# Where the last of five weight matrices made ahead is finished: in the mixer projection's second half, or behind the sixth query tile

## The chip, the core and the metric

The kernel runs on one core of a Trainium2 chip. The metric is the device time of one execution in microseconds; the time before is the median of three runs, 1076.35 us (1072.25 to 1078.3). TensorE multiplies matrices, VectorE (DVE) and ScalarE (ACT) work elementwise, GpSimd (POOL) does small vector work and issues some transfers, SyncE (SP) issues the other transfers. Each engine takes its instructions in one fixed order; an instruction that waits holds up all behind it on that engine.

## The reference

One layer of a hybrid decoder runs over 512 prompt tokens and 64 sample tokens (8 sequences of 8), 576 columns in all, with the same weights. All is float32.

```python
u = _rms(x) * g_pre_mix
proj = u @ w_in                                   # -> Mamba-2 heads and mLSTM heads
mix = jnp.concatenate([y_ssd, h_ml], axis=-1) @ w_out       # 2048 -> 1024
x = x + _rms(mix) * g_post_mix
u = _rms(x) * g_pre_x
qx = u @ w_xq                                     # 1024 -> 1024, 4 heads of 256
o = softmax(qx @ mem_k.T / 16) @ mem_v @ w_xo     # cross-attention on 256 memory rows
x = x + _rms(o) * g_post_x
u = _rms(x) * g_pre_ffn
x = x + _rms((silu(u @ w_gate) * (u @ w_up)) @ w_down) * g_post_ffn
```

For the prompt, `mem_k` and `mem_v` are made in the kernel from `mem_prompt` (normalised, times `w_mem_k`, `w_mem_v`); for the samples they come from a cache. The states of both recurrences are outputs too.

## The kernel before

**Numbers in two parts.** A float32 operand of a product is split in two: a rounded part made by a cast (`whi`, `..._h`), and the remainder made by a subtraction (`wlo`, `..._l`). A product takes three matmuls for each 128 rows of depth: high by high, high weight by low activation, low weight by high activation (L215, L216, L218 of `gemm`). A weight unit is 128 partitions by 1024 columns, 512 KB. `split_w` loads it (SP), casts it (ScalarE, L191) and lowers it (VectorE, sometimes GpSimd, L198); two raw buffers and three pairs of parts take turns.

**Blocks made ahead.** For eight weight units of later stages (`PRE`: two of `wxo`, and three each of `wgate` and `wup`) the remainder is made early, and kept in a DRAM tensor `pre`; the later stage fetches it from there into `wlo` (L1813). The first three units go through other code (`raw_ahead`, `low_ahead`, `store_ahead`). The last five go through `presplit(n, left)`: it finishes blocks until `left` are in flight, and starts `n` new ones. To start is a load `prel` on POOL's queue (L1326) into one of three buffers, which are shared with tiles of the attention (tags `pr`, `prl`, `mv`). To finish is a cast on ScalarE (`preh`, L1320), a subtraction in place on VectorE (`prel`, L1321) and a store on POOL's queue (`pre`, L1322). A block that takes a buffer again waits until the block before has been stored from it.

**The mixer projection's second half.** The output has eight tiles `j` of 128 features, over two groups of tokens: `i = 0`, 256 columns, and `i = 1`, 320 columns. `out2(j, i)` is the product with the second half of the depth, 24 matmuls. For `j` from 0 to 3 both groups are done; for `j` from 4 to 7 first the 320 columns of all four, then the 256 columns from 7 down to 4. The weight of `j = 4` is loaded anew for that. Each product's evacuation (`o2_evac`) adds it to `f` (VectorE, L1441, `f_mix` in the profile), squares the sum on ScalarE (`sq`, L302), adds that up in `ssqo` (VectorE, L303), and scales `f` (ScalarE, L1443). When the 320 columns of all eight tiles are there, `turned_cols` sums `ssqo` over the features (`ps_ss`, L249: three transposes on TensorE); it is queued behind `out2(7, 0)`. The root (`po_v` to `po_r`) and its spread over partitions (`ps_rb`, L287) follow, then `chain2`: norm, residual, and the parts `u2h`, `u2l` of the next activation. In this stage ScalarE and VectorE also prepare the memory rows (`memory`, with `ssqm` and the root `rmem`) and four weight units of the memory's products (`wm_split`). `presplit` is called once in each turn of `j`. A block's cast is queued behind the last evacuation so far (`evs[-1]`).

**The query stage.** `mem_key(3)` and `mem_value(3)` (`ps_mk`, `ps_v`) come first, then `xq(j, 1)` for `j` from 0 to 7: one unit of `wxq` against 320 columns, evacuated by `q_evac` (cast `qh` on ScalarE, L1555; remainder `ql` on VectorE, L1556; for the sample columns a copy `qsm`). Between the tiles stand `chain2` for the other token group, the squares of `x` (`pre_sums`) and two roots. Then comes the attention, head by head. `attn_values` writes the tiles `prh` and `prl`, which use the buffers of `preh` and of the last block `prel`.

**Order.** The program's order gives priorities. A planner with its own timeline simulation writes out each engine's order and assigns buffers; `tc.issue_after(ins)` forces what is traced in it behind `ins` on the same engine.

Of the kernel before, what the change touches and what calls it, by code (L numbers as in the profile page):

```python
# [115 lines left out]
def build(nc, tc, ctx, I, O):  # L116
    V, A, G, S, TE = nc.vector, nc.scalar, nc.gpsimd, nc.sync, nc.tensor
# [24 lines left out]
    def BP(name="b"):  # L142
        return pb.tile([P, 512], F32, name=name, tag="b")
# [77 lines left out]
    def gemm2(units, xh, xl, evac, name, halves=(0, 1), alloc=None, order=None, parts=HALVES):  # L221
        for i in halves:
            t0, n = parts[i]
            ps = (alloc or GP)(name)[:, :n]
            m = gemm(ps, units, xh, xl, t0, n, order=order)
            evac(t0, n, ps)
        return m

    def act(t):
        return lambda k, t0, n: t[:, k, t0:t0 + n]  # L230
# [48 lines left out]
    def rstd_rows(rc, chunks, out, alloc=None, copy=None):  # L279

        for c0 in range(0, len(chunks), 3):
            part = chunks[c0:c0 + 3]
            b = part[0][0]
            w = part[-1][0] + part[-1][1] - b
            ps = (alloc or BP)("ps_rb")
            for j, (t0, n) in enumerate(part):
                rows.append(TE.transpose(ps[:, t0 - b:t0 - b + n], rc[:n, c0 + j:c0 + j + 1].to_broadcast([n, P]),  # L287
                                         ident[:n, :n]))
            (copy or A.copy)(out[:, b:b + w], ps[:, :w])
        return ps  # L290
# [53 lines left out]
    for k in range(KT):  # L344
        if k % 2 == 0:
            c = slice(128 * k, 128 * k + 256)
# [64 lines left out]
    behind, split_behind = {}, {}  # L411
# [341 lines left out]
    for g in range(2):  # L753
        ps = BP("ps_xts")
# [5 lines left out]
    ps = BP("ps_bts")  # L760
# [15 lines left out]
    for g in range(2):  # L776
# [13 lines left out]
        for h in range(8):  # L790
            k, j = h % 2, (8 * g + h) // 2
# [6 lines left out]
    ps = BP("ps_eg")  # L798
# [7 lines left out]
    for b in range(4):  # L806
# [9 lines left out]
        for hb in range(2):  # L816
# [5 lines left out]
            for g in range(2):  # L822
                ps = BP("ps_hu")
# [6 lines left out]
    ps = BP("ps_yt")  # L830
# [206 lines left out]
    for hb in range(2):  # L1037
# [6 lines left out]
        for b in range(4):  # L1044
# [9 lines left out]
            for h in range(4):  # L1054
                ps = BP("ps_cu")
# [50 lines left out]
    def SL0(name, dt=F32R):  # L1106
        return big0.tile([P, KT, T], dt, name=name, tag="s0", bufs=1)
# [69 lines left out]
    evs = []  # L1177
# [116 lines left out]
    def ahead_src(n):  # L1294
        k, j = PRE[n]
        return I[{"xo": "wxo", "g": "wgate", "u": "wup"}[k]][j]
# [14 lines left out]
        with tc.issue_after(p_.low.ins):  # L1311
            S.dma_start(pre[:, n_, :], t_.bitcast(F32))

    def presplit(n, left):

        while len(ahead) > left:
            n_, t_ = ahead.pop(0)
            h_ = at.tile([P, 1024], F32R, name="preh", tag="prh", bufs=1)
            with tc.issue_after(evs[-1].ins):
                A.copy(h_, t_)  # L1320
            V.tensor_tensor(t_, t_, h_.bitcast(F32), op=ALU.subtract)  # L1321
            G.dma_start(pre[:, n_, :], t_)  # L1322
        for _ in range(n):
            n_ = turns.pop(0)
            t_ = at.tile([P, 1024], F32, name="prel", tag=("pr", "prl", "mv")[n_ % 3], bufs=1)
            G.dma_start(t_, ahead_src(n_))  # L1326
            ahead.append((n_, t_))
# [66 lines left out]
    def weights(key, src, n=1024, pool=None, cut=CUT, acc=False):  # L1394

        for kept in recent.values():
            for k, w in kept:
                if k == key:
                    return w
        kept = recent.setdefault(pool, [])  # L1400
        kept.append((key, split_w(src, n, cut, acc, pool)))
        if len(kept) > (NWX if pool else 3):
            kept.pop(0)
        return kept[-1][1]
# [9 lines left out]
    rmem_b = at.tile([P, 256], F32, name="rmem_b")  # L1414
    ssqm, ssq = ssq_tile("ssqm"), ssq_tile("ssqo")
    presplit(1, 0)
    for j in range(4):
        k2 = slice(2 * j, 2 * j + 2)
# [12 lines left out]
    def memory_norm(part, m):  # L1431
        with tc.issue_after(m.ins):
            if not part:
                rmem[0] = turned_cols(ssqm, CHUNKS[:2], "rmem", alloc=B1)
            else:
                rstd_rows(rmem[0], CHUNKS[:2], rmem_b, B1)
# [9 lines left out]
    def out2(j, i):  # L1446
        return gemm2([(*weights(("o", j), I["wout"][j, 1], cut=1024), KT)], act(mixm_h), act(mixm_l), o2_evac(j), "ps_o2", [i])
# [12 lines left out]
    def wm_split(i):  # L1460
        with tc.issue_after(loads[-1].ins):
            loads.append(S.dma_start(spare[i % 2], I["wmk"][6 + i] if i < 2 else I["wmv"][3][:, i - 2, :]))
        split(*wm[i], spare[i % 2])
# [8 lines left out]
    for j in range(4):  # L1472
        out2(j, 1)
        out2(j, 0)
        presplit(1, 1)
        if not j:
            store_ahead(*early_lows[2], pair_)
        memory(range(2 * j, 2 * j + 2))
        if j:
            wm_split(j - 1)  # L1480
    for j in range(4, 8):
        m = out2(j, 1)
        if j == 4:
            wm_split(3)
        presplit(0, 5 - j if j < 5 else 0)
        if j in (4, 6):
            memory_norm(j == 6, m)
    m = out2(7, 0)
# [56 lines left out]
    qh = SL0("qh")  # L1545
# [3 lines left out]
    def xq(j, i):  # L1549
        return gemm2([(*weights(("xq", j), I["wxq"][j], cut=1024 if i else CUT), KT)], act(u2h), act(u2l), q_evac(j), "ps_xq", [i])  # L1550

    def q_evac(j):
        def ev(t0, n, ps):
            c = slice(t0, t0 + 256)
            A.copy(qh[:, j, c], ps[:, 0:256])  # L1555
            V.tensor_tensor(ql[:, j, c], ps[:, 0:256], qh[:, j, c].bitcast(F32), op=ALU.subtract)  # L1556
            if t0:
                A.copy(qsm[:, j, :], ps[:, 256:320])
        return ev
# [136 lines left out]
    m = xq(5, 1)  # L1696
    with tc.issue_after(m.ins):
        rstd_rows(rc2[1][:, 2:3], HCHUNKS[1][2:], rb2, B1)
    m = xq(6, 1)
    with tc.issue_after(m.ins):  # L1700
        rc2[0] = rstd_cols([ssq2], HCHUNKS[0], "p20", alloc=B1)
# [322 lines left out]
    class Seven:  # L2024

        behind = ()
# [612 lines left out]
```

## Time and profile before

| what | value |
|---|---|
| median of three runs | 1076.35 us (1072.25 to 1078.3) |
| profiled execution, its time | 1079.62 us |
| its span, first to last instruction | 1077.7 us |
| mean granted TensorE clock | 0.995 |
| TensorE busy with matmuls | 99% of the span |
| VectorE, ScalarE, GpSimd busy | 72%, 57%, 22% |
| moved over the transfer queues | 184.10 MB, 171 GB/s in the mean |

Times in rows of the profile are microseconds from the start of the span; the durations in "ns" are so marked. PE is TensorE's matmul, PEld its weight load, SPq the queue of SyncE. Lines (L1320) are those of the kernel before. A product's name in the profile is that of its PSUM tile; the second half of the mixer projection appears as `ps_o`, as its first half does.

### The profile page before, as it was taken

How to read it: one execution, taken by the hardware profiler on the slowest of the kernel's cores; microseconds unless marked ns; L12 is line 12 of the kernel's file. 1: busy time of each engine (PE TensorE's matmuls, PEld its weight loads, DVE VectorE, ACT ScalarE, POOL GpSimd, SP SyncE). 2: the span in 40 equal slices, each digit the busy share in tenths (PEclk: the TensorE clock that was granted, in tenths of full speed). 3: DMA queues.
4: the chain of work that ended last, by engine and by line, in shares of the span. 5: the costliest groups of instructions: out<-in, count | busy, mean ns of one | idle time of the engine just before them, and what ended most of it. 6: DMA issues, size and time to landing. Idle time of an engine off the chain costs nothing.

```text
span 1077.7 us, 20671 instructions
## 1 busy us (share of the span) xinstructions
PE 1062.7 (99%) x8060; PEld 1009.2 (94%) x8060; DVE 775.5 (72%) x1554; ACT 617.4 (57%) x1115; POOL 239.1 (22%) x308
## 2 busy tenths in 40 slices
PE   9999999999999999989999999999999999999997
PEld 8999887778999999989999989999999999999997
DVE  6798775658878897758755556776567887787566
ACT  6778533345654566756545455646567566656654
POOL 0453543313213121110144301100011121111000
PEclk9999999999999999989999999999999999999999
DMA  6676544425655359773558775644486687578532
GB/s 208 168 166 134 158 127 177 147 88 168 196 148 154 83 165 250 264 260 121 170 192 291 269 257 173 236 145 96 128 180 146 153 197 173 119 191 187 142 122 88
DMA packets 59829, 184.10 MB, mean 171 GB/s; under 512 B 6700, under 2 KB 12204, under 8 KB 59220
## 3 DMA queue, kind: packets, MB, share of 16 engines
q1 hardware_dynamic: 43316, 139.79, 38.5%
q0 software_dynamic: 15840, 42.21, 20.5%
q8 instruction: 63, 1.03, 0.4%
q10 hardware_dynamic: 576, 0.79, 0.2%
q14 instruction: 34, 0.28, 0.1%
HBM read 162.11 MB, written 20.65 MB: 170 GB/s over the span
## 4 chain that ended last, share of the span: by engine, by line
PE 86%; DMA 7%; DVE 3%; issue 2%; ACT 1%; POOL 1%; SPq 0%; DVEq 0%; ACTq 0%; POOLq 0%
PE ps_in L218 6%; PE ps_in L215 6%; PE ps_in L216 6%; PE ps_v L882 5%; PE ps_g L2108 3%; PE ps_u L2108 3%; PE ps_g L2107 3%; PE ps_u L2109 3%; PE ps_g L2109 3%; PE ps_u L2107 3%; PE ps_dn L2107 2%; PE ps_dn L2109 2%; PE ps_dn L2108 2%; PE ps_dn L215 2%; PE ps_dn L218 2%
## 5 line engine op out<-in xcount | busy, mean ns | idle before, releaser
L215 PE MATMUL ps_in<-uh,whi 128*128 128x320 f32 (+1 forms) x544 | 162.4, 299 | 0.3 <-ACT la L477 0.3
L218 PE MATMUL ps_in<-uh,wlo 128*128 128x320 f32 (+1 forms) x544 | 162.0, 298 | 0.0
L216 PE MATMUL ps_in<-ul,whi 128*128 128x320 f32 (+1 forms) x544 | 161.2, 296 | 0.0
L191 ACT CAST whi<-raw 128x1024 fp32r<-128x1024 f32 (+1 forms) x98 | 99.1, 1012 | 83.4 <-PE ps_in L216 16.6
L198 DVE TENSOR_TENSOR wlo<-raw,whi 128x512 fp32r<-128x512 f32 (+2 forms) x91 | 88.0, 968 | 54.8 <-ACT whi L191 53.8
L215 PEld LDWEIGHTS ps_in<-uh,whi 128*128 128x128 f32 x544 | 102.2, 188 | 2.3 <-issue 0.8
L218 PEld LDWEIGHTS ps_in<-uh,wlo 128*128 128x128 f32 x544 | 102.1, 188 | 2.2 <-issue 1.3
L216 PEld LDWEIGHTS ps_in<-ul,whi 128*128 128x128 f32 x544 | 102.4, 188 | 0.5
L196 POOL DMA_DIRECT2D wlo<-win x31 | 27.4, 883 | 78.8 <-ACT wlo L195 68.3
L2107 PE MATMUL ps_g<-b,whi 128*128 128x288 f32 x144 | 42.4, 295 | 0.0
L2108 PE MATMUL ps_g<-b,whi 128*128 128x288 f32 x144 | 42.3, 294 | 0.0
L2108 PE MATMUL ps_u<-b,whi 128*128 128x288 f32 x144 | 42.2, 294 | 0.0
L2067 DVE TENSOR_TENSOR wlo<-sw,whi 128x1024 fp32r<-128x1024 f32 (+1 forms) x26 | 29.6, 1140 | 17.4 <-ACT whi L2066 17.4
L2107 PE MATMUL ps_u<-b,whi 128*128 128x288 f32 x144 | 42.2, 294 | 0.0
L2080 ACT CAST whi<-rawx 128x1024 fp32r<-128x1024 f32 (+1 forms) x26 | 25.6, 986 | 26.2 <-PE ps_dn L2108 13.3
L2057 ACT CAST whi<-raw 128x1024 fp32r<-128x1024 f32 (+1 forms) x26 | 25.6, 984 | 22.7 <-PE ps_g L2108 11.8
L215 PE MATMUL ps_xo<-qh,whi 128*128 128x288 f32 x128 | 38.3, 301 | 0.0
L215 PE MATMUL ps_o<-mixm_h,whi 128*128 128x256 f32 (+1 forms) x128 | 38.2, 298 | 0.0
L218 PE MATMUL ps_o<-mixm_h,wlo 128*128 128x256 f32 (+1 forms) x128 | 38.1, 299 | 0.0
L216 PE MATMUL ps_o<-mixm_l,whi 128*128 128x256 f32 (+1 forms) x128 | 38.1, 298 | 0.0
L216 PE MATMUL ps_xo<-ql,whi 128*128 128x288 f32 x128 | 37.7, 296 | 0.0
L215 PE MATMUL ps_xq<-u2h,whi 128*128 128x320 f32 (+1 forms) x128 | 37.4, 295 | 0.0
(828 smaller groups left out, 3901.8 us busy)
## 6 DMA issues: line engine op xcount, KB each, us to landing
raw<-win SPq DMA_DIRECT2D x35, 512.0 KB, 3.8
raw<-wout SPq DMA_DIRECT2D x14, 512.0 KB, 5.6
raw<-wxq SPq DMA_DIRECT2D x13, 512.0 KB, 5.5
raw<-wgate SPq DMA_DIRECT2D x13, 512.0 KB, 4.4
raw<-wup SPq DMA_DIRECT2D x13, 512.0 KB, 5.3
wlo<-win POOLq DMA_DIRECT2D x24, 256.0 KB, 5.5
kva<-vc SPq DMA_DIRECT2D x11, 512.0 KB, 6.3
raw<-wv SPq DMA_DIRECT2D x10, 512.0 KB, 4.0
```

The lines of the kernel that those rows point to most:

```text
L191: casts.append(A.copy(hi[:, :n], raw[:, :n]))
L196: accs.append(G.dma_start(lo[:, a:b], src[:, a:b], accum_op=ALU.add))
L198: e.tensor_tensor(lo[:, a:b], raw[:, a:b], hi[:, a:b].bitcast(F32), op=ALU.subtract)
L215: mm(ps, wh, ah, start=i == 0, stop=False)
L216: products.append(mm(ps, wh, al, start=False, stop=False))
L218: m = mm(ps, tiles[order[c]][1], xh(order[c], t0, n), start=False, stop=c == len(tiles) - 1)
L882: mm(ps, a, b, skip_group_check=True, **kw)
L2057: s.c1 = A.copy(s.h1[:, s.all], s.r1[:, s.all])
L2067: V.tensor_tensor(s.l2[:, s.all], sw[:, s.all], s.h2[:, s.all].bitcast(F32), op=ALU.subtract)
L2107: mm(ps, wh, b[0][k], start=start and k == 0, stop=False, skip_group_check=True)
L2108: mm(ps, wh, b[1][k], start=False, stop=False, skip_group_check=True)
L2109: m = mm(ps, wl, b[0][k], start=False, stop=k == nk - 1, skip_group_check=True)
```

## The change

At `j = 4` and later `presplit` is called with one block left in flight. So the block before the last one is still finished at `j = 4`, and the last one (unit 2 of `wup`) stays loaded and unfinished. It is finished by a new call, `presplit(0, 0, qev[-1])`, traced after `xq(5, 1)` and the row spread that follows it. Its cast is queued behind the newest evacuation cast `qh` of the query stage instead of behind one of the mixer's. For this, `presplit` takes an argument, and `q_evac` keeps its casts in a list. When and where the block is loaded isn't changed, nor what is computed.

```diff
-    def presplit(n, left):
+    def presplit(n, left, behind=None):
 
         while len(ahead) > left:
             n_, t_ = ahead.pop(0)
             h_ = at.tile([P, 1024], F32R, name="preh", tag="prh", bufs=1)
-            with tc.issue_after(evs[-1].ins):
+            with tc.issue_after((behind or evs[-1]).ins):
                 A.copy(h_, t_)
             V.tensor_tensor(t_, t_, h_.bitcast(F32), op=ALU.subtract)
             G.dma_start(pre[:, n_, :], t_)
...
         if j == 4:
             wm_split(3)
-        presplit(0, 5 - j if j < 5 else 0)
+        presplit(0, 1)
         if j in (4, 6):
             memory_norm(j == 6, m)
...
+    qev = []
+
     def q_evac(j):
         def ev(t0, n, ps):
             c = slice(t0, t0 + 256)
-            A.copy(qh[:, j, c], ps[:, 0:256])
+            qev.append(A.copy(qh[:, j, c], ps[:, 0:256]))
...
     m = xq(5, 1)
     with tc.issue_after(m.ins):
         rstd_rows(rc2[1][:, 2:3], HCHUNKS[1][2:], rb2, B1)
+    presplit(0, 0, qev[-1])
     m = xq(6, 1)
```

## The prediction

> **What bounds the kernel now.** I read the shares of the page first, then TensorE's own waits, longest first (us in total, times, longest), to see whether the busy engine has a hole anywhere.
>
> ```profile
> span 1077.7 us, 20671 instructions
> PE 1062.7 (99%) x8060; PEld 1009.2 (94%) x8060; DVE 775.5 (72%) x1554; ACT 617.4 (57%) x1115; POOL 239.1 (22%) x308
> ...
> PE ps_ss L249 <- DVE ssqo L303: 5.2, 1, 5.2
> ```
>
> TensorE sets the time, so an edit counts only through what it does to TensorE's holes and its clock. The longest is 5.2 us, once, where the sums over features `ps_ss` of the mixer output's last 320 tokens wait for their squares, summed up in `ssqo`. The chain of waits (start us, length us, what) says what that sum was late for:
>
> ```profile
> 451.88 4.00 DMA pre<-prel
> ...
> 458.61 5.52 DMA pre<-prel
> ...
> 464.42 10.65 DMA prel<-wup
> ...
> 475.15 1.05 ACT preh L1320
> ...
> 476.23 1.23 DVE prel L1321
> ...
> 477.79 0.40 DVE ssqo L303
> ...
> 478.26 0.40 DVE f_mix L1441
> ...
> 478.69 0.48 ACT sq L302
> ...
> 479.19 0.50 DVE ssqo L303
> ...
> 481.07 0.43 PE ps_rb L287 x2
> ```
>
> Read it backwards. The sums start when `ssqo` is done at 479.69; `ssqo` follows a square on ScalarE and the evacuation `f_mix` on VectorE, and these stood in their engines' order behind the lowering `prel` (L1321), which stood behind the cast `preh` (L1320), which waited for the last block made ahead, loaded for 10.65 us. That load could be issued only at 464.42, when an earlier block's store out of the same buffer had landed. The two engines' idle times in a timeline of the stage (start, length, engine, line, [idle before <- releaser]) confirm it:
>
> ```profile
> 475.15 1.04 ACT L1320 CAST preh<-prel 128x1024 fp32r<-128x1024 f32 x1 [9.15 <-DMA prel<-wup]
> ...
> 476.23 1.23 DVE L1321 TENSOR_TENSOR prel<-prel,preh 128x1024 f32<-128x1024 f32 x1 [8.94 <-ACT preh L1320]
> ```
>
> ScalarE and VectorE stand still for some 9 us each. TensorE goes on with products whose evacuation can wait, until it reaches the sums at 474.40.
>
> Then the price of the hole. The windows view gives busy time per stretch and, as the first number after POOL, the granted clock; the timeline gives the pace:
>
> ```profile
> 460.00:474.40 14.40, 14.40 (x109) 14.36 (x107) 6.94 (x12) 5.91 (x11) 1.75 (x4) 1.00 0.95 333
> 474.40:479.70 5.30, 0.16 (x2) 0.00 (x0) 2.94 (x7) 2.96 (x6) 1.25 (x2) 0.75 0.46 189
> 479.70:483.86 4.16, 4.12 (x20) 4.13 (x21) 3.10 (x9) 2.58 (x6) 0.83 (x1) 0.50 0.30 97
> ...
> 470.17 0.31 PE L218 MATMUL ps_o<-mixm_h,wlo 128*128 128x320 f32 x1
> 470.32 0.28 PE L215 MATMUL ps_o<-mixm_h,whi 128*128 128x256 f32 x1
> ...
> 474.29 0.28 PE L218 MATMUL ps_o<-mixm_h,wlo 128*128 128x256 f32 x1
> 479.74 0.90 PE L249 MATMUL ps_ss<-c,ssqo 128*128 128x128 f32 x3 [5.17 <-DVE ssqo L303]
> ...
> 489.15 0.28 PE L215 MATMUL ps_mk<-memhl,wmh 128*128 128x256 f32 x1
> 489.27 0.58 PE L287 MATMUL ps_rb<-c,po_r 128*128 128x128 f32 x3
> 489.77 0.39 PE L216 MATMUL ps_mk<-memhl,wmh 128*128 128x256 f32 x1
> ```
>
> After the hole the clock is 0.50 for 4.16 us. So the hole costs more than its 5.17 us.
>
> **The change, part by part.**
>
> *Removed from the mixer stage:* one cast (1.05 us, ScalarE), one lowering (1.23 us, VectorE), one store on POOL's queue, and the wait in front of them. What TensorE gets: from 470.32 to 474.29 it starts 36 matmuls of 256 columns, so 35 steps in 3.97 us, 0.1134 us each. The first 24 are the product `out2(7,0)`, the other 12 the head of `out2(6,0)`. Its next slot is 474.40; up to the first `ps_mk` at 489.15, 14.75 us, it still has the rest of `out2(6,0)` and `out2(5,0)` and `out2(4,0)`, 3 x 24 - 12 = 60 such matmuls, and five small transposes (three `ps_ss`, two `ps_rb`). The matmuls take 60 x 0.1134 = 6.80 us at the full clock. A transpose: three `ps_rb` push the next matmul from 489.26 to 489.77, 0.17 each; five make 0.85 us. Together 7.65 us, and **14.75 - 7.65 = 7.10 us** go away: 5.3 us of standing and 1.8 us of slow clock.
>
> *What is late next* at 474.40? The product `out2(7,1)` starts its last matmul at 470.17 and ends at about 470.48; evacuation, square and sum follow in the steps that the chain shows (478.17 or so to 479.69, 1.5 us), so `ssqo` is there at about 472.0, 2.4 us before TensorE asks. The steps behind (`po_v`, the power on POOL, `ps_rb`) are paced by TensorE's own products and keep their distance. The loads of `x` need their row, with the time to landing under it, and so do the stage that uses them and its first product:
>
> ```profile
> L1451 SPq DMA_DIRECT2D x<-xT x1: 424/424/424, 463.4 to 463.4; - x1
> DMA to landing us min/median/max: 7.5/9.8/12.2
> ...
> 503.34 0.54 DVE L1375 SCALAR_TENSOR_TENSOR u2l<-x,par,u2h 128x320 fp32r<-128x320 f32 x1
> 504.70 0.31 PE L216 MATMUL ps_xq<-u2l,whi 128*128 128x320 f32 x1
> ```
>
> They land by 463.4 + 12.2 = 475.6 at the latest; VectorE's first use, just behind the `ps_rb` copy of 489.27, comes no earlier than 482 after a shift of 7.1. From there VectorE works nearly without a break up to the last `u2l` (done at 503.88, read at 504.70, 0.8 us to spare). This run starts from `ps_rb`, which TensorE releases, so both shift together and the 0.8 us stay.
>
> *Put into the query stage* behind the first evacuation of the sixth tile (`xq(5,1)`): the same three instructions. Their rows, and those around their new place (times as before the change):
>
> ```profile
> L1320 ACT CAST preh<-prel x5: 1038/1039/1048, 449.3 to 475.1; 128x1024 fp32r<-128x1024 f32 x5
> L1321 DVE TENSOR_TENSOR prel<-prel,preh x5: 1225/1226/1227, 450.4 to 476.2; 128x1024 f32<-128x1024 f32 x5
> L1322 POOL DMA_DIRECT2D pre<-prel x5: 531/538/543, 451.9 to 477.7; - x5
> 520.00:530.00 10.00, 10.00 (x71) 10.00 (x70) 9.04 (x27) 6.17 (x18) 0.96 (x1) 1.00 0.85 288
> ...
> 523.41 0.37 ACT L1555 CAST qh<-ps_xq 128x256 fp32r<-128x256 f32 x1
> 524.98 0.42 ACT L302 ACTIVATE sq<-x 128x256 f32<-128x256 f32 x1 [1.08 <-DVE ssq L303]
> 526.91 0.37 ACT L1555 CAST qh<-ps_xq 128x256 fp32r<-128x256 f32 x1 [1.50 <-PE ps_xq L218]
> ...
> 524.81 1.22 DVE L198 TENSOR_TENSOR wlo<-raw,whi 128x1024 fp32r<-128x1024 f32 x1
> 527.00 0.31 PE L218 MATMUL ps_xq<-u2h,wlo 128*128 128x320 f32 x1
> ```
>
> The operand is there by then (landed at 475), so the cast waits for nothing: 1.04 us into an idle ScalarE (1.08 us, then 1.50 us). On VectorE the lowering can start at about 524.8, in a stretch that is 90% full. The nearest reader is the eighth tile's low weight, made at 524.81 to 526.03 and used by TensorE at 527.00: 0.97 us of slack. Behind it, the lowering costs TensorE nothing. In front, the cost is 1.23 - 0.97 = 0.3 us at least; if VectorE also waits for the cast, about 1.7 us. The extreme is a cast that is queued only behind the evacuation of 526.91: ready at 528.3, lowered by 529.5, the weight at 530.8, 3.8 us late. Bounds 0 and 3.8. I take 0, as the weight is ready (its cast is older) when the lowering's operand is not. The store is 0.5 us of POOL, which has under 1 us of work in that stretch, and 512 KB more on queues that are not TensorE's bound there. Its buffer is next written in the attention (row at rival D). The reader of the stored block, the up-projection, is two stages later.
>
> *Sum:* the profiled execution took 1079.62 us around a span of 1077.7; 1079.62 - 7.10 = 1072.5. The median of the runs is 1076.35, 3.27 below the profiled one. The hole is a wait inside every execution, so I take it off the median too: **1076.35 - 7.1 = 1069.2 us**, 0.66% faster.
>
> **Rivals.** About 0.5%, 5.4 us, is what a measurement can tell from no change; faster means below 1071.0, slower above 1081.7.
>
> A. *The hole is longer in the profiled execution than in the timed ones.* It hangs on a transfer that took 10.65 us with the DMA share at 0.95; the runs spread from 1072.25 to 1078.3. If the whole 3.27 us lie here, the timed hole costs 3.8 us and the time is 1072.5. Against it: nothing shows where the 3.27 us lie.
>
> B. *The lowering gets in front of the eighth weight.* Cost 1.7 to 3.8 us as above: 1070.9 to 1073.0. For it: VectorE has no reserve there. Against it: the readiness named.
>
> C. *The change moves the block but not the wait:* something else, such as the fourth `wout` weight or the memory's root, holds TensorE for as long at the same place: 1076.4. Against it: of all waits around the place only the chain through `preh` is long.
>
> D. *Slower: the store lands too late.* The buffer of the moved block is handed to the attention's `prl`:
>
> ```profile
> L203 DVE TENSOR_TENSOR prl<-ps_pt,prh x8: 678/686/692, 553.5 to 626.7; 128x512 fp32r<-128x512 f32 x8
> ...
> 450.00:460.00 10.00, 10.00 (x76) 10.00 (x75) 9.53 (x16) 8.57 (x16) 1.62 (x3) 1.00 0.73 256
> ```
>
> Until the store has read it, `prl` may not be written at 553.5, VectorE stands, and TensorE after it. A store issued at about 527.6 that landed at 564 would cost some 10.5 us: 1079.8. It decides from a landing 7.1 us past the slot, at 560.6, that is 33 us after issue. Against it: the store of 451.88 in the chain took 4.00 us, with VectorE at 9.53 of 10. The Trainium skill, "SBUF — State Buffer", section "SBUF: two separate sides", speaks for this rival: a transfer issued from GpSimd needs its descriptors written by GpSimd, which some VectorE operations lock out for as long as they last. By that rule the store would be slowest just where VectorE is fullest, as in its new place. The row of 451.88 does not bear it out at this size.
>
> **How the numbers follow.** The forecast 0.55 (its own range 1066 to 1072, for the spread of medians), A 0.20, B 0.12, C 0.07, D 0.06. Range 1065.5 to 1074.5: it takes in the forecast, B and most of A, over eight tenths. Faster by over 0.5%: nearly all of the forecast's 0.55 and a little of A and B, 0.58; slower 0.04, the worse part of D; within 0.5% the rest, 0.38.
>
> **What would show it.** Right: no wait of `ps_ss` for `ssqo`; no slice of clock below 1.00 near 480; ScalarE and VectorE without their 9 us; `ps_mk` starting at about 482; `preh` last seen near 517, straight behind a `qh`, with a short or no wait. The gain is kept if `ps_xq` ends 7 us earlier and nothing later is longer. Wrong: a new wait of `ps_xq` for `wlo` (B), `prl` waiting for the store (D), a hole at 474 with another name (C), or a hole gone with the time hardly moved (A).

## The result, and the profile after

The changed kernel takes 1071.8 us in the median of 11 executions (1070.67 to 1073.69). The kernel before, timed beside it, takes 1079.02 us (1070.02 to 1081.64). The ratio is 0.9944 with a 95% interval of 0.9921 to 0.9967: 0.56% faster, and a second timing gave 0.995 (0.992 to 0.9981). The predicted 1069.2 us is 2.6 us low. The time lies inside the stated range and the sign was right.

TensorE's waits after the change (us in total, times, longest), longest first; they are all that the view lists:

```profile
span 1069.8 us, 20670 instructions
PE 1060.1 (99%) x8060; PEld 1006.9 (94%) x8060; DVE 775.2 (72%) x1554; ACT 616.5 (58%) x1115; POOL 236.9 (22%) x308
...
PE ps_warm L337 <- DVE wz L334: 1.1, 1, 1.1
PE ps_in L378 <- ACT uh L361: 0.7, 1, 0.7
PE ps_rb L1858 <- DVE px_r L1851: 0.6, 1, 0.6
PE ps_ss L241 <- DVE ssqx L303: 0.3, 1, 0.3
```

The wait of `ps_ss` for `ssqo` is gone, and no wait of its size has taken its place. The windows of the stage (busy time of TensorE, of its weight loads, of VectorE, ScalarE and POOL, then the granted clock, the DMA share, GB/s):

```profile
460.00:474.40 14.40, 14.40 (x109) 14.39 (x108) 9.82 (x22) 9.26 (x18) 2.46 (x5) 1.00 0.92 321
474.40:479.70 5.30, 5.30 (x49) 5.30 (x48) 4.50 (x11) 2.51 (x5) 0.85 (x1) 1.00 0.74 247
479.70:482.00 2.30, 2.30 (x22) 2.22 (x21) 0.97 (x1) 1.88 (x3) 0.00 (x0) 1.00 0.57 216
```

TensorE is full where it stood for 5.30 us, and its clock is 1.00 where it was 0.50. In the first window ScalarE works 9.26 us in place of 5.91 and VectorE 9.82 in place of 6.94: the two standstills are over. The timeline at the former hole and at the new place:

```profile
471.42 0.49 DVE L303 TENSOR_TENSOR ssqo<-ssqo,sq 128x320 f32<-128x320 f32 x1 [0.27 <-ACT sq L302]
...
474.18 0.49 PE L249 MATMUL ps_ss<-c,ssqo 128*128 128x128 f32 x3
...
481.67 0.28 PE L215 MATMUL ps_mk<-memhl,wmh 128*128 128x256 f32 x1
...
516.32 1.07 ACT L1320 CAST preh<-prel 128x1024 fp32r<-128x1024 f32 x1
...
517.33 1.22 DVE L198 TENSOR_TENSOR wlo<-raw,whi 128x1024 fp32r<-128x1024 f32 x1
518.86 1.21 DVE L1321 TENSOR_TENSOR prel<-prel,preh 128x1024 f32<-128x1024 f32 x1
...
519.51 0.31 PE L218 MATMUL ps_xq<-u2h,wlo 128*128 128x320 f32 x1
520.38 0.59 POOL L1322 DMA_DIRECT2D pre<-prel  x1 [4.51 <-DVE prel L1321]
```

`ssqo` is done at 471.91, 2.3 us before the sums start; the moved lowering stands behind the eighth weight's. How long the product stage is now, and whether the gain is kept, shows in two rows of tile views (how often, then least, median and longest duration in ns, then the first and the last start). Of the kernel before:

```profile
L215 PE MATMUL ps_o<-mixm_h,whi x128: 276/304/563, 426.5 to 488.8; 128*128 128x320 f32 x64, 128*128 128x256 f32 x64
...
L215 PE MATMUL ps_xq<-u2h,whi x128: 276/304/395, 501.4 to 599.0; 128*128 128x320 f32 x64, 128*128 128x256 f32 x64
```

Of the kernel after:

```profile
L215 PE MATMUL ps_o<-mixm_h,whi x128: 275/304/363, 426.3 to 481.3; 128*128 128x320 f32 x64, 128*128 128x256 f32 x64
...
L215 PE MATMUL ps_xq<-u2h,whi x128: 275/304/395, 493.9 to 591.5; 128*128 128x320 f32 x64, 128*128 128x256 f32 x64
```

The stage `ps_o` shrank from 62.3 us (488.8 - 426.5) to 55.0, by 7.3. The query products end 7.5 us earlier, so nothing is given back in their stage. The span is 7.9 us shorter in all.

### The profile page after: what moved, and what is told of

Read it like the earlier page. It is cut to its first block, busy times and chain, and to the rows that moved or that the text cites. A ratio compares the mean times of both kernels' runs of the same rounds, so it can differ in the third digit from the quotient of the medians.

```text
span 1069.8 us, 20670 instructions
## 1 busy us (share of the span) xinstructions
PE 1060.1 (99%) x8060; PEld 1006.9 (94%) x8060; DVE 775.2 (72%) x1554; ACT 616.5 (58%) x1115; POOL 236.9 (22%) x308
## 4 chain that ended last, share of the span: by engine, by line
PE 96%; DVE 2%; DMA 1%; issue 0%; ACT 0%; SPq 0%; POOL 0%; DVEq 0%; POOLq 0%
PE ps_in L218 7%; PE ps_in L215 7%; PE ps_in L216 6%; PE ps_v L882 5%; PE ps_g L2111 3%; PE ps_u L2111 3%; PE ps_g L2110 3%; PE ps_u L2112 3%; PE ps_g L2112 3%; PE ps_u L2110 3%; PE ps_dn L2110 2%; PE ps_dn L2112 2%; PE ps_dn L2111 2%; PE ps_dn L215 2%; PE ps_dn L218 2%; PE ps_o L218 2%
## 5 line engine op out<-in xcount | busy, mean ns | idle before, releaser
L198 POOL TENSOR_TENSOR wlo<-raw,whi 128x512 fp32r<-128x512 f32 x17 | 29.9, 1764 | 38.1 <-ACT whi L191 38.0
```

The costliest lines, as they stand in the source:

```text
L198: e.tensor_tensor(lo[:, a:b], raw[:, a:b], hi[:, a:b].bitcast(F32), op=ALU.subtract)
```

## The experiments

The theory is the prediction's: TensorE waits because a block is finished in VectorE's and ScalarE's order ahead of the sums while its load is late; neither the work of the cast and the lowering nor their place costs anything. The rivals to be told apart: the work itself is the price; the new place has a price of its own; the load is late by its own length, whatever runs beside it. And it was open where the 2.6 us of the forecast went. Each ratio compares executions of the altered kernel with executions of the kernel before, timed beside them on the same chip. The length of the stage `ps_o` is taken as in the two rows above.

### The block in a buffer of its own

```diff
-            t_ = at.tile([P, 1024], F32, name="prel", tag=("pr", "prl", "mv")[n_ % 3], bufs=1)
+            t_ = at.tile([P, 1024], F32, name="prel", tag="kvc" if n_ == 7 else ("pr", "prl", "mv")[n_ % 3], bufs=1)
...
-    kv = [... at.tile([P, 1024], F32, name="kvc")]
+    kv = [... at.tile([P, 1024], F32, name="kvc", tag="kvc", bufs=1)]
```

This starts from the kernel before and leaves everything where it was; only the load no longer has to wait for a store.

> The kernel before, with one buffer more for the last block: it is loaded into the buffer of a later cache tile, so its load need not wait for an earlier block's store. Cast, lowering and store stay where they were, in the mixer projection's second half. Theory (the price is the wait for the load, on two engines that work in order): the load is issued some 10 us earlier, the cast starts at about 466 without a wait, the sums ps_ss wait for nothing, the clock near 480 stays 1.00, and the time is that of the changed kernel, 1071 to 1073 us. Rival (the price is the work itself, 2.3 us of ScalarE and VectorE in that stage, or the place of the cast): the hole stays, wholly or for the larger part, and the time stays at 1077 to 1080.

Measured: 1072.43 us (1070.1 to 1073.93), ratio 0.9961 (0.9932 to 0.999), stage 55.0 us (426.5 to 481.5). The load is issued by 434.7, some 30 us earlier than before and not 10. The last block's cast in the timeline, and the two windows:

```profile
466.37 1.05 ACT L1320 CAST preh<-prel 128x1024 fp32r<-128x1024 f32 x1 [0.32 <-DVE prel L1321]
```

```profile
460.00:474.40 14.40, 14.40 (x109) 14.39 (x108) 11.23 (x24) 10.26 (x18) 2.48 (x5) 1.00 0.93 326
474.40:479.70 5.30, 5.30 (x49) 5.30 (x49) 4.56 (x11) 2.91 (x6) 0.85 (x1) 1.00 0.72 255
```

Cast and lowering are still in this stage, VectorE is busier than after the change (11.23 against 9.82 us), and TensorE has no hole. The wait is the price, not the work, and not its place either once the load is in time.

### The block finished two products later, still in the same stage

```diff
-        presplit(0, 5 - j if j < 5 else 0)
+        presplit(0, 0 if j == 7 else 1)
```

> The kernel before, with the last block finished two products later: behind the evacuation of the eighth tile's 320 columns, still inside the mixer projection's second half. The load is as late as before (lands at about 475), so ScalarE still stands still for it, from about 472 to 475, and VectorE behind it. Theory (only what stands ahead of the sums counts): the squares are all summed by 472, the sums start at about 474.3 without a wait, no slow clock, 1071 to 1074 us. Rival (any standing of the two engines in this stage is paid for by TensorE, through the evacuations and the weight of out2(4,0)): a hole of 2 to 5 us a little later, 1075 to 1079 us.

Measured: 1071.9 us (1070.7 to 1075.96), ratio 0.9972 (0.9947 to 0.9998), stage 55.0 us. ScalarE's wait and POOL's wait for the buffer:

```profile
ACT preh L1320 <- DMA prel<-wup: 2.9, 1, 2.9
...
POOL prel L1326 <- DMA pre<-prel: 9.1, 2, 5.1
```

The load is as late as before (10.7 us to landing) and ScalarE still stands for it, 2.9 us. TensorE does not (0.2 us at a `ps_rb` is all): the squares that its sums need are no longer behind the cast. So a standstill of the two engines costs nothing by itself; it costs when the squares are queued behind it.

### The last load issued twice

```diff
-            G.dma_start(t_, ahead_src(n_))
+            for _ in range(2 if n_ == 7 else 1):
+                G.dma_start(t_, ahead_src(n_))
```

> The kernel before, with the last block loaded twice into the same buffer, one load after the other; the values are the same. Theory: the cast waits for the second landing, some 4.5 to 6 us after the first (the nearest load that nothing collides with, that of the block before, took 4.4 us), and the whole delay goes into the hole: 10 to 11 us in place of 5.2, and as the slow clock after it does not grow with the hole, the time is 4.5 to 6 us above the kernel before of the same call. Rival (something else is late at 479 as well, the load only one of several): the time moves by less than 2 us.

Measured: 1073.39 us (1070.03 to 1081.62), ratio 0.9984 (0.9951 to 1.0016). The expectation missed. The kernel's instruction order is planned from the program, the plan saw the second load, and it put the cast behind the squares, at 487.0. The hole of the profiled execution (1081.62 us) has another name:

```profile
PE ps_rb L287 <- DVE rmem_r L276: 2.7, 1, 2.7
```

The timeline of POOL shows where it comes from:

```profile
478.37 0.53 POOL L1327 DMA_DIRECT2D prel<-wup  x1 [6.92 <-DMA prel<-wup]
```

The second load had to wait on POOL for the first one into the same buffer, which took 10.6 us. The memory's root (`rmem_y`, on POOL) stood behind it, VectorE waited 5.9 us for the root, and TensorE for VectorE. This was meant as a double dose of the same wait and was none. It shows another path from a late landing to TensorE, the one that is met again below where the cast and the lowering are left out. The stage took 59.5 us, 4.5 more than 55.0: 2.7 us of standing, and 3.4 us at a clock of 0.50 behind it.

### The loads of x held back

```diff
-    S.dma_start(x[:, 0:4, :], I["xT"][:, 0:4, :])
-    S.dma_start(x[:, 4:8, :], I["xT"][:, 4:8, :])
...
+    for a in (0, 4):
+        A.copy(x[:, a, 256:257], f[:, 7, 256:257])
+        S.dma_start(x[:, a:a + 4, :], I["xT"][:, a:a + 4, :])
```

The two loads of `x`, 1152 KB each, now follow a column that is written only when the last 320-column product, `out2(7,1)`, has been evacuated.

> The kernel before, with the two loads of x (2.3 MB) held back: a copy of one column, which the load then overwrites, makes them wait for the last evacuation of the eighth tile's 320 columns, at about 471.5 in place of 463.0. The last block and its finishing stay as before. Theory (the block's load is slow because the loads of x run beside it): it lands 4.5 to 6 us after its issue, at about 469 to 470.5, the hole is gone or under 1 us, x lands by about 482, before VectorE first needs it, and the time is 1071 to 1074 us. Rival (the load is slow by itself or through the stores on its own queue): it still takes 8 to 11 us and the hole stays at 3 to 5 us, 1077 to 1080 us.

Measured: 1073.12 us (1071.54 to 1074.78), ratio 0.997 (0.9948 to 0.9992), stage 55.0 us. The two loads in the timeline, and the issues (KB, us to landing):

```profile
460.78 0.53 POOL L1326 DMA_DIRECT2D prel<-wup  x1 [2.87 <-DMA pre<-prel]
...
471.00 0.80 SPq L1488 DMA_DIRECT2D x<-xT  x2
...
prel<-wup POOLq DMA_DIRECT2D x1, 512.0 KB, 4.6
```

Without `x` beside it the block's load lands in 4.6 us where it took 10.65, and cast and lowering are done long before the sums, in their old place. But this execution doesn't show by itself that holding `x` back did it. The earlier block's store had landed in time for the load to be issued at 460.78, ahead of the moment at which `x` is issued otherwise (about 1 us behind `raw<-wxq`, here issued at 460.66), and a load that is issued ahead of `x` can land in 5 us with `x` in its usual place too (see below). What speaks for `x` are the times: all ten executions took under 1075 us, while 18 of the 31 of the kernel before beside them took longer. So holding `x` back takes the hole away; that the load is late because `x` runs beside it fits with this and isn't shown directly. The later `x` has a price: from the first `ps_xq` to the first `ps_at` it is 39.4 us against 38.8 after the change.

### The change with the cast and the lowering left out

Three forms of the changed kernel ask what the new place costs. In the first the moved block is stored as it was loaded:

```diff
-            with tc.issue_after((behind or evs[-1]).ins):
-                A.copy(h_, t_)
-            V.tensor_tensor(t_, t_, h_.bitcast(F32), op=ALU.subtract)
+            if not behind:
+                with tc.issue_after(evs[-1].ins):
+                    A.copy(h_, t_)
+                V.tensor_tensor(t_, t_, h_.bitcast(F32), op=ALU.subtract)
```

> The changed kernel with the moved cast and the moved lowering left out: the store writes the whole weight block in place of its remainder, so the second term of that unit is not what the reference needs. Theory (the instructions lie in gaps of ScalarE and behind the eighth weight on VectorE, and cost TensorE nothing): within 0.8 us of the changed kernel of the same call. Rival (the lowering delays something that TensorE waits for): 1.5 to 3.8 us faster than the changed kernel.

Measured: 1077.15 us (1070.27 to 1079.72), ratio 0.9997 (0.9963 to 1.0031). It has less work and is slower than the change (1071.18 us beside it), which neither the theory nor its rival had foreseen. The waits of three engines in its profiled execution show why:

```profile
POOL pre L1323 <- DMA prel<-wup: 8.9, 1, 8.9
...
DVE rmem_a L274 <- POOL rmem_y L273: 7.9, 1, 7.9
...
PE ps_rb L287 <- DVE rmem_r L276: 4.7, 1, 4.7
```

The cast had held the store at its place. Without it the plan put the store on POOL's queue in front of the root `rmem_y` that the mixer stage needs, and it was issued at 474.94. POOL waited 8.9 us for the same late load, VectorE for POOL, TensorE for VectorE; the stage was 62.5 us. The same landing was paid for through a third engine's queue.

The second form is the first with the store held behind the last root on POOL:

```diff
+            with tc.issue_after(pows[-1].ins) if behind else ExitStack():
+                G.dma_start(pre[:, n_, :], t_)
```

> The changed kernel with the moved cast and lowering left out, and the store of the raw block queued on POOL behind the power of the query stage's root, near its place in the changed kernel; the second term of that unit is then not what the reference needs. Theory (in no_finish it was the store, ahead of the memory's root on POOL's queue and waiting for the load, that kept the hole; and the cast and the lowering cost TensorE nothing at their new place): no hole, and within 0.8 us of the changed kernel, 1070.5 to 1073 us. Rival 1 (leaving out the cast and the lowering was what lost the gain): 1076 us or more. Rival 2 (the two cost TensorE what they take on VectorE): 1069 to 1070 us.

Measured: 1071.32 us (1070.18 to 1076.86), ratio 0.9972 (0.9944 to 1.0), stage 55.0, and 38.8 us from the first `ps_xq` to the first `ps_at`, as with the change. Cast and lowering at the new place therefore cost nothing that can be told, and the store's place was the cause in the first form. (Two of the ten executions took 1076.04 and 1076.86 us; why isn't known.) The load took 10.2 us here, and nobody waited for it.

The third form moves the finish of the changed kernel from the sixth query tile to the third (`presplit(0, 0, qev[-1])` behind `xq(2,1)`), where VectorE still has to lower three more weights of the query stage behind it.

> The changed kernel with the last block finished three query tiles earlier, behind the newest qh cast after xq(2, 1): its lowering stands in the run of VectorE instructions (residual adds of the second token group) which has no gap, ahead of two weights' lowerings. Theory (what the place costs is decided by the slack of the weights behind it, 0.97 us for the eighth one): the weights come up to 1.2 us later, TensorE waits for a wlo for 0 to 0.5 us, the time is 0 to 1 us above the changed kernel of the same call. Rival (any place behind the mixer stage is free): no wait and no difference; the other rival (VectorE is the bound in this stretch and passes on all of the work): 1.2 us or more slower, with waits of ps_xq.

Measured: 1072.43 us, ratio 0.997 (0.9939 to 1.0002); one execution of 2166.66 us, twice the others, is not in the ratio, and its cause is not known. The timeline of VectorE, and one row of TensorE's weight loads:

```profile
509.37 1.22 DVE L1321 TENSOR_TENSOR prel<-prel,preh 128x1024 f32<-128x1024 f32 x1
511.51 1.22 DVE L198 TENSOR_TENSOR wlo<-raw,whi 128x1024 fp32r<-128x1024 f32 x1
513.65 1.22 DVE L198 TENSOR_TENSOR wlo<-raw,whi 128x1024 fp32r<-128x1024 f32 x1
...
519.36 1.22 DVE L198 TENSOR_TENSOR wlo<-raw,whi 128x1024 fp32r<-128x1024 f32 x1
...
520.63 0.19 PEld L218 LDWEIGHTS ps_xq<-u2h,wlo 128*128 128x128 f32 x1 [0.32 <-DVE wlo L198]
```

In front of the weights the lowering does cost something. Counted from the first `ps_xq` (494.8 here, 493.9 after the change), the three weights come 1.1 us later than after the change. The eighth one, lowered from 519.36, is late by more than its slack, and its weight load waits 0.3 us for it. From `ps_xq` to `ps_at` it takes 39.1 us against 38.8, longer by as much. The theory held.

### Two more transfers behind x

The kernels before that were timed beside these runs spread from 1070 to 1082 us, the changed ones from 1070 to 1074. To stretch the block's load, two copies of 512 KB within DRAM were queued on SP right behind `x`, once in the kernel before and once in the changed one:

```diff
-    S.dma_start(x[:, 4:8, :], I["xT"][:, 4:8, :])
+    xd = S.dma_start(x[:, 4:8, :], I["xT"][:, 4:8, :])
+    crowd = dr.tile([P, 2, 1024], F32, name="crowd")
+    for n in range(2):
+        with tc.issue_after(xd.ins):
+            S.dma_start(crowd[:, n, :], I["wgate"][20 + n])
```

> The kernel before, with two copies of 512 KB each from a weight to a scratch tensor in DRAM queued right behind the loads of x: 1 MB read and 1 MB written that nobody waits for, beside the last block's load. Theory (the hole is the block's landing, moved by what runs beside it): in the profile the load takes 12 to 15 us in place of 10.65 and the hole grows by the same 1.5 to 4 us, to 7 to 9; executions without a hole become rare, and the median is 2 to 4 us above that of the kernel before in the same call. Rival (the landing is at its limit already, or what runs behind x does not touch it): load 10 to 11 us, hole 5 to 6, median equal.

> The changed kernel with the same two copies at the same place. Theory (nothing waits for the block's landing any more, and x has some 6 us to spare): no hole, 1071 to 1073.5 us, as the changed kernel without the copies. Rival (the stage is bound by its transfers, the change only moved the place): a wait for x or a weight, 1074 us or more.

Measured, in the kernel before: 1071.57 us (1070.2 to 1083.58), ratio 0.9996 (0.9957 to 1.0034); in the changed kernel: 1072.33 us, ratio 0.9968 (0.9942 to 0.9994). For the kernel before the expectation missed: its profiled execution, 1073.07 us, has no hole at all, and a stage of 55.0 us. Its timeline and the issue:

```profile
462.84 0.53 POOL L1326 DMA_DIRECT2D prel<-wup  x1 [2.87 <-DMA pre<-prel]
...
463.69 0.33 SPq L1450 DMA_DIRECT2D x<-xT  x1
...
prel<-wup POOLq DMA_DIRECT2D x1, 512.0 KB, 5.0
```

The block's load was issued 0.85 us ahead of `x`, not behind it, and landed in 5.0 us. That is the piece that the prediction lacked. Of the ten executions two took 1080.67 and 1083.58 us and the other eight at most 1073.75: they fall into two groups, as those of the kernel before do. In the changed kernel the expectation came true; there is no hole.

### More profiled executions of the two kernels

The changed kernel was timed again, and the kernel before was profiled twice more, with these expectations:

> The changed kernel once more, beside the two that follow, for comparison with them on one chip: 1070.5 to 1073.5 us, no wait of ps_ss for ssqo.

> The kernel before once more, for a second look at one execution with its time. Theory (the kernel before spreads over 1070 to 1082 us because the landing of the last block's load moves against the sums): the hole at ps_ss, with 1.5 to 2 us of slow clock if it is over some 3.4 us, accounts for this execution's distance from about 1071.8 us; an execution near 1072 us shows no hole. Rival (the spread lies elsewhere): the hole is about 5 us whatever the time.

> A third look at one execution of the kernel before. Theory: its time is 1071.8 us plus the hole and, for a hole over some 3.4 us, 1.5 to 2 us of slow clock. Rival: the hole does not go with the time.

Measured: 1071.18 us for the changed kernel (1070.31 to 1073.41), with a stage of 55.0 us; 1078.97 and 1078.95 us for the kernel before, with a hole in both. From the lists of waits of these two executions of the kernel before:

```profile
PE ps_ss L249 <- DVE ssqo L303: 5.9, 1, 5.9
```

```profile
PE ps_ss L249 <- DVE ssqo L303: 5.4, 1, 5.4
```

Both executions lie 7.2 us above 1071.8, and their holes of 5.9 and 5.4 us with 1.5 to 2 us of slow clock come to 6.9 to 7.9 us. That fits the theory but doesn't test it, since no execution near 1072 us was among them.

The two profiled executions of the changed kernel show the load both ways. The first:

```profile
464.93 0.53 POOL L1326 DMA_DIRECT2D prel<-wup  x1 [5.90 <-DMA pre<-prel]
...
462.90 0.33 SPq L1450 DMA_DIRECT2D x<-xT  x1
...
prel<-wup POOLq DMA_DIRECT2D x1, 512.0 KB, 10.1
```

And the second:

```profile
460.85 0.53 POOL L1326 DMA_DIRECT2D prel<-wup  x1 [2.92 <-DMA pre<-prel]
...
461.73 0.33 SPq L1450 DMA_DIRECT2D x<-xT  x1
...
prel<-wup POOLq DMA_DIRECT2D x1, 512.0 KB, 4.9
```

It is one program with two outcomes: in the first the earlier block's store was late, POOL stood 5.90 us for it, and the load came 2.03 us behind `x`; in the second POOL stood 2.92 us, and the load came 0.88 us ahead. All profiled executions in which one load of the block waits for that store, ordered by the time from the issue of `x` to the issue of the load:

| kernel | load issued against x, us | load to landing, us | hole of `ps_ss` for `ssqo`, us |
|---|---|---|---|
| before, `x` held back | -10.22 | 4.6 | none |
| changed, two copies more | -1.00 | 4.8 | none |
| changed, second profile | -0.88 | 4.9 | none |
| before, two copies more | -0.85 | 5.0 | none |
| changed, behind the third query tile | -0.24 | 9.0 | none |
| changed, stored as loaded, store held | -0.09 | 10.2 | none |
| before, finished two products later | +1.27 | 10.7 | none |
| before, third profile | +1.32 | 11.0 | 5.4 |
| before, first profile | +1.39 | 10.65 | 5.2 |
| changed, stored as loaded | +1.93 | 10.5 | none (4.7 of `ps_rb`) |
| changed, first profile | +2.03 | 10.1 | none |
| before, second profile | +2.11 | 10.6 | 5.9 |

A lead of 0.85 us or more over `x` goes with a landing in about 5 us; a lead of 0.24 us or less, or none, goes with 9 to 11. Whether that makes a hole is up to what is queued behind the cast.

## Why the prediction was right, and where it was wrong

**The wait and its price: right.** The chain from `ssqo` back to the load was the right one. The buffer of its own removes its first link and has no hole, the later finish removes its last link and has none. The price was put at 7.10 us; the stage is 7.3 us shorter, and the first `ps_mk` comes 7.48 us earlier (489.15 to 481.67), 0.2 of it from the earlier start of the stage. The 14.75 us from the wait to `ps_mk` were to become 7.65; they are 7.49 (474.18 to 481.67). That the hole costs more than its length because the clock is 0.50 after it holds too: the stage is 7.3 us shorter for a wait of 5.17, and 5.17 with half of the 4.16 us at 0.50 make 7.25. The Trainium skill, "TensorE: Matmul & The Clock Gate", section "Part 1: The HAM clock gate (the "warmup" mystery)", says that the clock drops to half after an idle window of some 3.4 us and comes back after about as long a busy time. The traces agree in part. The clock fell to 0.50 not at the end of the hole but 2.5 us after TensorE had stopped, and stayed there for 6.8 us, of which 4.16 lie behind the hole. In the other two profiled executions of the kernel before and in the first form without cast and lowering it fell some 2 to 4 us after TensorE had stopped, and again stayed for 6.8 us. With the load issued twice, a standing of only 2.72 us was followed by 3.4 us at 0.50. So the slow stretch lasted 3.4 us or twice that, and a standing of 2.72 us was enough to set it off.

**What is late next: right.** `ssqo` was expected at about 472.0 and is done at 471.91. C, another wait at the same place, would have shown as a hole at 474; TensorE is full there. The last activations kept only half of their 0.8 us: the last `u2l` is done at 496.82 and read at 497.21, since VectorE's run shifted by 7.1 us and the query products by 7.5. "Both shift together" was not quite so; nobody waited for it.

**The new place: right.** The lowering was put at 0, with bounds 0 and 3.8. It stands behind the eighth weight's, as forecast, and the form without cast and lowering has the same time from `ps_xq` to `ps_at`. B did not happen. What the prediction says of a lowering in front of the eighth weight, 1.23 - 0.97 = 0.3 us at least, came out where it was put there: 0.3 us. The cast was forecast near 517 behind a `qh` and is at 516.32, straight behind one.

**D, the slower one: not seen.** The store was issued at 520.38 and landed in 4.4 us, from the view of issues around it:

```profile
pre<-prel POOLq DMA_DIRECT2D x1, 512.0 KB, 4.4
```

It landed about 21 us before `prl` is first written, at 546.0, so D had a distance of nearly five times the transfer. VectorE was busy for 10.00 of the 10 us up to 520 and for 1.97 of the next 2 us, in which the store was issued. By the rule cited for D (the Trainium skill, "SBUF — State Buffer", section "SBUF: two separate sides") the store would be late there, if these are operations that lock GpSimd out, which no run shows; neither the issue (0.59 us against 0.54 before) nor the landing shows a delay.

**The base of the sum: wrong.** The step that failed is "The hole is a wait inside every execution, so I take it off the median too." The gain is that of an execution with the hole. By their times the kernel before has executions without it too: in its four timings it was under 1075 us in 34 of 92 executions (2 of 11, 13 of 31, 8 of 25, 11 of 25), while all 21 of the changed kernel lie between 1070.31 and 1073.69. The median of three, 1076.35, stood between the two kinds, and the whole 7.1 us were taken from it once more. The sum from the profiled execution, 1079.62 - 7.10 = 1072.5, stood in the text, and it is the one that came true: the profiled execution after takes 1071.59 us, the median is 1071.8. That 1071.8 lies inside the stated range is owed to the range's upper part, which was there for A and B; it lies above 1071.0, where "faster" was to begin from the base of 1076.35.

So A's time, 1072.5, was the nearest of all, but its mechanism was only half right. In A the hole is shorter in the timed executions than in the profiled one; by the runs it is mostly there in full or not at all, as it goes with how early the load is issued against `x`. Two things remain inference. No profile caught the unaltered kernel before without its hole. That its 1070 to 1073 us are such executions rests on the kernel with two copies more, which had no hole at 1073.07 us, and on the changed kernel, which shows both orders of the loads without any addition. The mean granted clock, on record for each of 81 executions of the kernel before in its three later timings, supports it: it is 0.998 in the mean of the 27 under 1074 us, as in the changed kernel, and 0.995 in the mean of the 41 over 1077 us, as in the profiled one with its hole. A stretch of 6.8 us at 0.50 in a span of 1077 us makes just this difference of 0.003. And some of the executions before lie between the two groups (8 of the 81 from 1075 to 1077 us, with a clock of 0.997 in the mean); whether these have a shorter hole was not seen.

**The sign and its size.** "Nothing shows where the 3.27 us lie", the prediction says against A. Its profile held a hint of it: `x` issued at 463.03 and 463.40, the load at 464.42, and a spread of 6 us over three runs of a kernel whose work never varies. Since the kernel before is bimodal, the measured gain depends on how many of its executions had the hole: its medians in the four timings are 1079.02, 1076.02, 1078.47 and 1076.05 us. By the medians alone, 1071.8 us is 0.67% below the first and 0.39% below the second (an estimate, as the changed kernel wasn't timed beside the second). So it is partly luck that the measured gain comes near the forecast 0.66%: nine of the eleven executions beside it took over 1075 us. What the change does dependably is to make the time indifferent to that race: its first profile has the late load (10.1 us) and no hole. No variant is better than the change: own buffer, later finish, held store and the change itself lie within 1071.2 to 1072.5 us, which their intervals do not separate.

## What to carry to other kernels

When an engine's hole begins with a transfer, look in the engines' orders for what is queued behind the instruction that waits: moving that instruction, giving its load a free buffer, or holding back the transfers beside it took away the hole and its 7 us of the stage, and a store planned early on a third engine's queue brought them back. Before a gain read from one profiled execution is taken off a median, look whether the runs form one group: subtract from the profiled execution's own time if the wait hangs on a race. An instruction can be what keeps a later one in its place, so leave it out of an experiment only together with a look at where the rest has gone.

## What the runs showed of the hardware

A load of 512 KB on POOL's queue landed in 4.6 to 5.0 us when it was issued 0.85 us or more ahead of the two loads of `x` (2.3 MB) on SP's queue, and in 9.0 to 11.0 us when it was issued 0.24 us ahead or later; `x` itself (median of its two loads) took 9.4 to 11.5 us in all of these but the one where it was held back (6.5). The Trainium skill, "DMA: Bandwidth & Descriptors", section "Queues, rings and completion order", says that each DMA engine takes turns between the queues that it has work for, a packet at a time. The late loads fit with turns of that kind. That a lead of under a microsecond goes with 5 us for a load that needs 4.6 us without `x` beside it was not expected. No run here shows how the packets were ordered, and none set the lead on its own with all else equal: lead and landing go together in twelve profiles, and that the one causes the other is inference.

Whether the load comes ahead or behind goes with the store in front of it. POOL stood for 2.87 to 2.92 us in the four executions with the early load, 3.7 us in the two in between, and 5.06 to 5.90 us in those with the late one. The store was issued 3.1 to 3.5 us ahead of SP's next load (`raw<-wxq`) in all of them. In those with the early load it has landed at about the moment that load is issued (the block's load follows it at 460.85, against 460.72, in the changed kernel's second profile); in the others it is still under way then, and in the six with the latest load also when `x` is issued; that it shares the transfer engines with them is inference. What tips it was not seen: the copies that were added come after both, so they cannot be the cause, and the changed kernel went both ways without them.
